# A causal mask for attention scores, set by a minimum on VectorE instead of by products on TensorE

## The chip, the core and the metric

The kernel runs on one core of a Trainium2 chip. It is one launch, and its time is that of the device, in microseconds (us), as the median of several runs. Five engines work side by side, each through its own queue in order: TensorE (PE in the profile, with its weight loads as PEld), VectorE (DVE), ScalarE (ACT), GpSimd (POOL) and SyncE (SP, which issues the loads from memory). They wait for each other through semaphores. TensorE writes its results into PSUM, which has eight banks; all other operands are in SBUF.

## The reference

The program is a decoder trunk of two layers on 256 tokens of width 1024. Each layer is a half-step SwiGLU block, a token mixer and another half-step SwiGLU block, with a norm and a modulation by a condition vector ahead of each. The mixer of the first layer is stick-breaking attention with 16 heads of 64; that of the second is a recurrent block. The change is in the attention alone:

```python
z = jnp.einsum('bhqd,bhkd->bhqk', q[:, :, t0:L], k[:, :, :L])
mask = s_idx[None, :] < t_idx[:, None]
log_keep = jnp.where(mask, jax.nn.log_sigmoid(-z), 0.0)
later = lax.cumsum(log_keep, axis=3, reverse=True) - log_keep
w = jnp.where(mask, jnp.exp(jax.nn.log_sigmoid(z) + later), 0.0)
```

A key that is not earlier than its query gets the weight zero and adds nothing to the running sum. In the kernel both follow when such a score is -1e30: softplus of it is zero, and so is the exponential at the end.

## The kernel before

**Numbers.** Matrix products are made in float32r, with each operand split into a rounded high part and the rest: `wh`, `wl` for weights, two tiles of `hx` for activations. A product is three matmuls (high by high, high by low, low by high), 128x256 results each, and nearly all come from one line, L613 in `group`. ScalarE makes the high part of a weight tile (L584) and VectorE the low part (L587), from a raw tile that SyncE has loaded (`load`).

**Order.** The program is first recorded as a list of operations (`pr.op`), each with an engine, an estimated cost, and the buffers it reads and writes. `Program.schedule` then plays the list through with these costs and decides the order on each engine, and `Space.fit` which bank or tile a buffer gets. So a cost that is changed can move instructions that nothing else in the diff touches. `SCORES` and `VALUES` are the costs given to the score products and the values products.

**Attention** (`attention`) treats the 16 heads as four sets of four heads, c = 0 to 3. Its order is written out by hand as a list of stages: projections of queries and keys (`q`), of values (`v_proj`), then per set `scores`, `sums` and `values`. A set has four score banks, two for each of e = 0, 1. A bank with i = 0 holds scores of the first key block against all 256 queries, for two heads; one with i = 1 holds those of the second key block against the second 128 queries. Keys lie on the partitions, queries along the columns.

For one set the stages follow each other like this:

1. `scores`: per bank one mask product on TensorE (L1104): identity by a mask tile of zeros and -1e30 in bf16, with start=True. It writes the 256 columns where the key block meets the same query block, and the score products (L1119, eight of them on 64 rows of the array) add to it.
2. `softplus`: ScalarE takes absolute values of the banks (two per e, as each bank is ready), an exponential and a logarithm; VectorE adds the positive part of the bank (L1134); then `split` rounds the result into high and low parts, on ScalarE and on VectorE (L877).
3. `sums`: TensorE adds running sums into the same banks, by a triangular matrix (L1149) and, for i = 0, a matrix of minus ones (L1152); ScalarE takes the exponential, which is the weights.
4. `values`: TensorE multiplies weights and values (L1173, on 64 columns of the array); ScalarE and VectorE (L1179) round the result into two parts for the output projection `down`.

Between the stages of a set TensorE has projections of other sets, so that ScalarE and VectorE get time for step 2. VectorE is also given the modulation work: for each tile of the modulation weights, loaded by SyncE into one of four tiles `rawm`, a multiplication with a sum (L647, in `mod_tile`), spread over the blocks by a hook.

At the start of the program GpSimd and VectorE build the constants: `ident`, `ntri`, `none_` and `mask`, which is 256 columns of bf16 (the same 128 columns twice).

Of the kernel before, what the change touches and what calls it, by code (L numbers as in the profile page):

```python
# [14 lines left out]
P = 128  # L15
# [26 lines left out]
KICK0, COPIED, PLAIN = (1, 4), (7,), 2  # L42
HXPAD, HKPAD, ARPAD = 112, 16, 56
SKIP = 1
SCORES = 1400.0
VALUES = 1350.0

OFF_NG = 0
OFF_MB = OFF_NG + 6 * KD
# [359 lines left out]
def trunk(ctx, tc, first_in, cb, par, modw, gu, wdn, qk, wv, wo, win, wri, wout, out):  # L409
# [107 lines left out]
    none_ = fixed("none", P, F32R)  # L517
    dve.tensor_copy(none_, t32[:, P:])
    ident = fixed("ident", P, BF16)
    mask = fixed("mask", T, BF16)  # L520
    pool.affine_select(at[1][:, :P], ones, [[1, P]], ALU.is_equal, 0.0, base=0, channel_multiplier=-1)
    dve.tensor_copy(ident, at[1][:, :P])
    pool.memset(at[2], 0.0)
    for o in (0, P):
        pool.affine_select(at[2][:, o : o + P], at[2][:, o : o + P], [[1, P]], ALU.is_gt, NEG,
                           base=0, channel_multiplier=-1)
    dve.tensor_copy(mask, at[2])
    for t in xbt:
        pool.memset(t[:, 0:4], 0.0)
    mraw, mfin = {}, {}  # L530
# [482 lines left out]
    def attention(l, s, nxt, hook):  # L1013
# [77 lines left out]
        def scores(c):  # L1091
# [3 lines left out]
            pairs = [qs.pop(f) for f in fs]  # L1095
            for e in range(2):
                zs[c, e] = Buf(banks), Buf(banks)

            def masked(b, i):
                def fn():  # L1100
                    diag, m = b()[:, :T], mask
                    if i == 0:
                        diag, m = first(b()), mask.rearrange("p (f t) -> p f t", f=2)
                    pe.matmul(diag, ident, m, start=True, stop=False, skip_group_check=True)  # L1104
                pr.op("PE", c_mm(T, 1), fn, [], [b])

            for e in range(2):
                for i in range(2):
                    masked(zs[c, e][i], i)
            zb = [zs[c, e] for e in range(2)]  # L1110

            def products():

                for j, y in enumerate(pairs):
                    for i, (kc, qc) in enumerate(((slice(T, T + P), slice(0, T)), (slice(T + P, 2 * T), slice(P, T)))):
                        m = NC[i] // 2
                        for e in range(2):
                            rows = slice(e * 64, (e + 1) * 64)
                            pe.matmul(zb[e][i]()[:, j * m : (j + 1) * m], y()[rows, kc], y()[rows, qc], start=False, stop=j == 1,  # L1119
                                      skip_group_check=True)  # L1120

            pr.op("PE", SCORES, products, pairs, [z for zz in zb for z in zz])
            for e in range(2):
                softplus(c, e)

        def softplus(c, e):
# [434 lines left out]
```

## Time and profile before

| | |
|---|---|
| time, median of 3 runs (lowest to highest) | 948.97 us (948.61 to 949.02) |
| the profiled execution: its own time | 950.72 us |
| the profiled execution: span from first to last instruction | 949.0 us |
| mean granted TensorE clock | 0.996 |
| busy: TensorE, VectorE, ScalarE, GpSimd | 938.7, 777.7, 558.9, 2.4 us |
| attention's four score sets, by the mask products | 217.4 to 272.1 us |
| read from memory | 248.92 MB, 263 GB/s over the span |

A row of the timeline gives the start in the span, the length from the first start to the last end, engine, line, operation, tiles out and in, and how many instructions of one kind it holds; a bracket names idle time before it and who ended it. The length of a matmul reaches to the end of its pipeline, so a step on TensorE is read from start to start. A row of the groups gives busy time, the mean length of one in ns, and the idle time ahead of it. A row of the waits names who waited for whom, the total, how often, and the longest. A row of busy time by stage gives, after the stretch and its length, one figure for each engine, then the granted clock, the share of the load engines and GB/s.

### The profile page before, as it was taken

To read this page: it belongs to the slowest core of one execution; us is meant where nothing else is said; L and a number is where in the kernel's file an instruction comes from. 1 tells how busy PE (TensorE), PEld (TensorE's weight loads), DVE (VectorE), ACT (ScalarE), POOL (GpSimd) and SP (SyncE) were. 2 spreads that over 40 slices of the span, in tenths; PEclk is the share of its full clock that TensorE was granted. 3 is DMA by queue.
4 is the path that set the end of the run, shared out by engine and by line. 5 is a ranking of instruction groups with operands and counts; after the bars stand their busy time and mean duration, and the time that the engine had idled before them with its cause. 6 is when DMAs were issued, how large, how long until landed. Compare 5 with 4: busy or idle time off the path is not lost.

```text
span 949.0 us, 19623 instructions
## 1 busy us (share of the span) xinstructions
PE 938.7 (99%) x8094; PEld 927.0 (98%) x8094; DVE 777.7 (82%) x1264; ACT 558.9 (59%) x914; POOL 2.4 (0%) x15
## 2 busy tenths in 40 slices
PE   8999999999999999999999999999999999999997
PEld 6999999999999999999999999999999999999996
DVE  8999988899777998888889998866999997555443
ACT  6785454488775755454367555535789676544343
POOL 1000000000000000000000000000000000000000
PEclk9999999999999999999999999999999999999999
DMA  9989989949643699889967999885253546555431
GB/s 364 404 319 354 346 337 353 365 173 350 235 155 134 242 340 367 311 319 349 362 236 288 344 348 340 333 331 228 90 185 127 223 174 241 208 181 204 171 113 45
DMA packets 48332, 251.25 MB, mean 265 GB/s; under 512 B 5361, under 2 KB 5745, under 8 KB 28530
## 3 DMA queue, kind: packets, MB, share of 16 engines
q1 hardware_dynamic: 47952, 249.59, 69.4%
q8 instruction: 63, 1.03, 0.4%
q10 hardware_dynamic: 290, 0.40, 0.1%
q14 instruction: 27, 0.22, 0.1%
HBM read 248.92 MB, written 1.05 MB: 263 GB/s over the span
## 4 chain that ended last, share of the span: by engine, by line
PE 97%; DMA 1%; DVE 1%; ACT 0%; SPq 0%; DVEq 0%; issue 0%
PE bank L613 90%; PE bank L1044 2%; PE bank L919 1%; PE bank L1279 1%; DMA raw<-in_gu 1%; DMA arenar<-in_first_in 1%; PE bank L1119 1%; PE bank L1173 1%; PE bank L1149 1%; DVE wl L587 0%; DVE arenar L647 0%; DVE x L1391 0%; PE bank L1152 0%; PE bank L1104 0%; PE bank L706 0%; PE bank L698 0%
## 5 line engine op out<-in xcount | busy, mean ns | idle before, releaser
L613 PE MATMUL bank<-hx,wh 128*128 128x256 f32 (+1 forms) x3264 | 560.4, 277 | 0.0
L584 ACT ACTIVATE wh<-raw 128x1024 fp32r<-128x1024 f32 (+1 forms) x330 | 335.3, 1037 | 285.0 <-PE bank L613 196.3
L613 PEld LDWEIGHTS bank<-hx,wh 128*128 128x128 f32 x3264 | 493.3, 188 | 0.0
L587 DVE TENSOR_TENSOR wl<-raw,wh 128x1024 fp32r<-128x1024 f32 (+1 forms) x330 | 387.0, 1196 | 125.6 <-ACT wh L584 121.8
L613 PE MATMUL bank<-hx,wl 128*128 128x256 f32 (+1 forms) x1640 | 452.7, 277 | 0.0
L613 PEld LDWEIGHTS bank<-hx,wl 128*128 128x128 f32 x1640 | 308.4, 188 | 0.0
L613 PE MATMUL bank<-arenar,wh 128*128 128x256 f32 x1696 | 289.8, 276 | 0.0
L613 PEld LDWEIGHTS bank<-arenar,wh 128*128 128x128 f32 x1696 | 255.7, 188 | 0.2 <-issue 0.2
L613 PE MATMUL bank<-arenar,wl 128*128 128x256 f32 x848 | 234.5, 276 | 0.1
L647 DVE SCALAR_TENSOR_TENSOR rawm<-rawm,cact 128x1024 f32<-128x1024 f32 x128 | 154.8, 1220 | 6.3 <-DMA rawm<-in_modw 5.8
L613 PEld LDWEIGHTS bank<-arenar,wl 128*128 128x128 f32 x848 | 159.3, 188 | 0.3 <-DVE wl L587 0.3
L556 ACT ACTIVATE arenar<-a 128x256 fp32r<-128x256 f32 x88 | 35.2, 405 | 9.8 <-DVE a L872 7.9
L877 DVE TENSOR_TENSOR arenar<-a,arenar 128x256 fp32r<-128x256 f32 x88 | 36.5, 419 | 0.5 <-ACT arenar L556 0.5
L556 ACT ACTIVATE sg<-bank 128x256 f32<-128x256 f32 x82 | 30.0, 369 | 10.2 <-PE bank L613 10.2
L872 DVE TENSOR_TENSOR a<-bank,sg 128x256 f32<-128x256 f32 x82 | 34.1, 419 | 1.6 <-ACT sg L556 1.4
L556 ACT ACTIVATE arenaf<-bank 128x256 f32<-128x256 f32 (+1 forms) x53 | 23.3, 487 | 12.5 <-PE bank L613 5.1
L787 DVE SCALAR_TENSOR_TENSOR x<-bank,mf,x 128x256 f32<-128x256 f32 (+1 forms) x49 | 21.7, 474 | 9.3 <-PE bank L613 9.1
L556 ACT ACTIVATE hx<-x,mf 128x256 fp32r<-128x256 f32 x40 | 19.2, 499 | 16.5 <-DVE x L787 16.5
L556 ACT ACTIVATE hx<-hpre,mf 128x256 fp32r<-128x256 f32 x41 | 20.0, 503 | 11.4 <-DVE hpre L733 10.5
L1044 PE MATMUL bank<-wh,hx 128*128 128x256 f32 x128 | 23.0, 279 | 0.0
L647 DVE SCALAR_TENSOR_TENSOR arenar<-arenar,cact 128x1024 f32<-128x1024 f32 x16 | 19.4, 1221 | 1.9 <-DMA arenar<-in_first_in 1.9
L1501 ACT ACT_TABLE_LOAD x15 | 19.2, 1283 | 1.6 <-PEq L1549 1.3
(126 smaller groups left out, 506.5 us busy)
## 6 DMA issues: line engine op xcount, KB each, us to landing
raw<-in_gu SPq DMA_DIRECT2D x79, 1024.0 KB, 5.3
rawm<-in_modw SPq DMA_DIRECT2D x128, 512.0 KB, 6.8
raw<-in_wdn SPq DMA_DIRECT2D x44, 1024.0 KB, 5.1
raw<-in_win SPq DMA_DIRECT2D x10, 1024.0 KB, 4.8
arenar<-in_first_in SPq DMA_DIRECT2D x16, 512.0 KB, 8.4
raw<-in_qk SPq DMA_DIRECT2D x8, 1024.0 KB, 5.0
raw<-in_wout SPq DMA_DIRECT2D x5, 1024.0 KB, 4.8
raw<-in_first_in SPq DMA_DIRECT2D x8, 512.0 KB, 9.3
```

Of the source, the lines that this page charges most:

```text
L556: act.activation(o(), i(), f, **{k: (v() if callable(v) else v) for k, v in kw.items()})
L584: act.activation(h()[:, :m], raw()[:, a : a + m], AF.Copy)
L587: dve.tensor_tensor(lo()[:, :m], raw()[:, a : a + m], f32(h()[:, :m]), ALU.subtract)
L613: pe.matmul(o(b()), wc(u()), xc(v()), start=start and n == 0, stop=stop and n == len(passes) - 1, skip_group_check=True)
L647: dve.scalar_tensor_tensor(raw(), raw(), 1.0, cact(), ALU.mult, ALU.mult, accum_out=m()[:, t : t + 1])
L787: dve.scalar_tensor_tensor(x[d]()[:, w], acc.b()[:, j * T + w.start : j * T + w.stop], gate()[:, d : d + 1], x[d]()[:, w], ALU.mult, ALU.add)
L872: V(lambda: dve.tensor_tensor(a(), b()[:, T:], sg(), ALU.mult), T, [(b, (1, 0)), sg], [a])
L877: V(lambda: dve.tensor_tensor(y[1](), a(), f32(y[0]()), ALU.subtract), n, [a, y[0]], [y[1]])
L919: pr.op("PE", c_mm(T, 4), lambda: pe.matmul(b()[:, g * T : (g + 1) * T], raw()[:, c0 : c0 + P], h0(), start=start, stop=False, skip_group_ ...
L1044: pe.matmul(o, u()[:, tb * P : (tb + 1) * P], v()[:, c0 : c0 + 256], start=start and n == 0, stop=k == KD - 1 and n == 2, skip_group_check ...
L1119: pe.matmul(zb[e][i]()[:, j * m : (j + 1) * m], y()[rows, kc], y()[rows, qc], start=False, stop=j == 1, skip_group_check=True)
L1501: act.preload_act_table_set(TABLES[t])
```

## The change

The mask products are gone. The score products now begin the banks themselves (start=True on the first of the two heads of each bank). When a set's products are done, VectorE takes a minimum in place, bank by bank, of the 256 columns and a mask tile, which holds 1e30 where the key is earlier and -1e30 elsewhere. The mask tile is 128 columns of float32, read twice by an access pattern, and is built with one selection and no cast. The banks are still taken at the same place in the list, by operations on TensorE that cost nothing and issue nothing. `SCORES` and `VALUES` are each 50 larger.

```diff
-SCORES = 1400.0
-VALUES = 1350.0
+SCORES = 1450.0
+VALUES = 1400.0
...
-    mask = fixed("mask", T, BF16)
+    mask = fixed("mask", P)
...
-    pool.memset(at[2], 0.0)
-    for o in (0, P):
-        pool.affine_select(at[2][:, o : o + P], at[2][:, o : o + P], [[1, P]], ALU.is_gt, NEG,
-                           base=0, channel_multiplier=-1)
-    dve.tensor_copy(mask, at[2])
+    pool.memset(mask, -NEG)
+    pool.affine_select(mask, mask, [[1, P]], ALU.is_gt, NEG, base=0, channel_multiplier=-1)
...
-            def masked(b, i):
-                def fn():
-                    diag, m = b()[:, :T], mask
-                    if i == 0:
-                        diag, m = first(b()), mask.rearrange("p (f t) -> p f t", f=2)
-                    pe.matmul(diag, ident, m, start=True, stop=False, skip_group_check=True)
-                pr.op("PE", c_mm(T, 1), fn, [], [b])
-
-            for e in range(2):
-                for i in range(2):
-                    masked(zs[c, e][i], i)
+                for b in zs[c, e]:
+                    pr.op("PE", 0.0, lambda: None, [], [b])
+
...
-                            pe.matmul(zb[e][i]()[:, j * m : (j + 1) * m], y()[rows, kc], y()[rows, qc], start=False, stop=j == 1,
+                            pe.matmul(zb[e][i]()[:, j * m : (j + 1) * m], y()[rows, kc], y()[rows, qc], start=j == 0, stop=j == 1,
...
             for e in range(2):
+                for i in range(2):
+                    b = zs[c, e][i]
+
+                    def masked(b=b, i=i):
+                        o = first(b()) if i == 0 else b()[:, :T].rearrange("p (f t) -> p f t", f=2)
+                        dve.tensor_tensor(o, o, mask.unsqueeze(1).to_broadcast([P, 2, P]), ALU.min)
+                    V(masked, T, [b], [b])
                 softplus(c, e)
```

What the schedule makes of it is seen in the order of the instructions. Line numbers after the change are smaller by 3 ahead of the stage `scores` and by 5 behind it; the score products, L1119, become L1107: L613 becomes L610, L647 L644, L1134 L1129, L877 L874, L1149 L1144, L1152 L1147, L1173 L1168.

TensorE, shortly behind the values products of the second set, where the running sums of the third come (banks 69 and 70 hold the first key block of e = 0 and e = 1; `hk` and `hx` are the activations of a projection of the last queries and keys). Before:

```order
L613 MATMUL bank_68<-hk_95,wh_79 128x256
L613 MATMUL bank_68<-hk_96,wh_79 128x256
L613 MATMUL bank_68<-hk_95,wl_86 128x256
L613 MATMUL bank_68<-hx,wh_79 128x256 x2
L613 MATMUL bank_68<-hx,wl_86 128x256
L613 MATMUL bank_68<-hx,wh_79 128x256 x2
L613 MATMUL bank_68<-hx,wl_86 128x256
L1149 MATMUL bank_69<-arenar_2524,ntri 128x512 x2
```

And now, from the same group on:

```order
L610 MATMUL bank_68<-hk_95,wh_79 128x256
L610 MATMUL bank_68<-hk_96,wh_79 128x256
L610 MATMUL bank_68<-hk_95,wl_86 128x256
L1144 MATMUL bank_69<-arenar_2520,ntri 128x512 x2
L1147 MATMUL bank_69<-arenar_2520,none 128x2x128 x2
L1144 MATMUL bank_65<-arenar_2520,ntri 128x256 x2
L610 MATMUL bank_68<-hx,wh_79 128x256 x2
L610 MATMUL bank_68<-hx,wl_86 128x256
L1144 MATMUL bank_70<-arenar_2520,ntri 128x512 x2
```

(A like group on `hk` stands ahead of the first row shown in both.) Two groups of three matmuls that stood ahead of the first half of the sums now stand behind it, and the second half comes after one further group instead of three. In the fourth set the sums move the other way: the first half two groups later, the second half one.

VectorE, from the last modulation passes ahead of the third set to the end of that set's softplus (`rawm` are modulation tiles, `wl` low parts of weights, bank 69, 65, 70 and 64 the set's score banks). Before:

```order
L647 SCALAR_TENSOR_TENSOR rawm_76,mr_165<-rawm_76,cact 128x1024
L647 SCALAR_TENSOR_TENSOR rawm_77,mr_165<-rawm_77,cact 128x1024
L587 TENSOR_TENSOR wl_89<-raw_73,wh_82 128x1024
L662 TENSOR_TENSOR mr_167<-mr_167,x 128x8
L665 SCALAR_TENSOR_TENSOR mf_168<-mr_167,x 128x8
L1020 TENSOR_TENSOR lam<-lam,nlam 128x10
L1022 TENSOR_SCALAR psp<-lam 128x10
L1021 TENSOR_SCALAR nsp<-lam 128x10
L587 TENSOR_TENSOR wl_90<-raw_71,wh_83 128x1024
L1134 SCALAR_TENSOR_TENSOR arenaf_2525<-bank_69,arenaf_2525 128x512
```

And now:

```order
L644 SCALAR_TENSOR_TENSOR rawm_75,mr_161<-rawm_75,cact 128x1024
L659 TENSOR_TENSOR mr_163<-mr_163,x 128x8
L662 SCALAR_TENSOR_TENSOR mf_164<-mr_163,x 128x8
L1117 TENSOR_TENSOR bank_69<-bank_69,mask 128x2x128
L1117 TENSOR_TENSOR bank_65<-bank_65,mask 128x256
L1117 TENSOR_TENSOR bank_70<-bank_70,mask 128x2x128
L1117 TENSOR_TENSOR bank_64<-bank_64,mask 128x256
L584 TENSOR_TENSOR wl_90<-raw_71,wh_83 128x1024
L644 SCALAR_TENSOR_TENSOR rawm_76,mr_161<-rawm_76,cact 128x1024
L1129 SCALAR_TENSOR_TENSOR arenaf_2521<-bank_69,arenaf_2521 128x512
```

The four minima stand in one piece, directly ahead of a weight split and the softplus additions. Since the first set two modulation passes have moved from ahead of this point to behind it (ten instead of twelve stand ahead, counted from the first set's score products), and the three small passes on `lam` have moved to the first set. SyncE's queue follows: the loads of modulation tiles stand later among the loads of `qk` and `wo` weights.

## The prediction

> **What bounds the kernel now.** I read the page first, then the wait view of TensorE, then the busy time by stage around attention.
>
> ```profile
> span 949.0 us, 19623 instructions
> PE 938.7 (99%) x8094; PEld 927.0 (98%) x8094; DVE 777.7 (82%) x1264; ACT 558.9 (59%) x914; POOL 2.4 (0%) x15
> ...
> PE 97%; DMA 1%; DVE 1%; ACT 0%; SPq 0%; DVEq 0%; issue 0%
> ```
>
> TensorE (PE) is busy for 938.7 of 949.0 us and makes up 97% of the chain that ended last. VectorE (DVE) is busy 82% of the time, so it has room on average, but an average says nothing about attention.
>
> ```profile
> PE bank L919 <- DVE hpre L738: 2.1, 1, 2.1
> PE bank L1412 <- POOL eps L509: 1.2, 1, 1.2
> ```
>
> This is the whole wait view of TensorE: 3.3 us, and L1412 and L919 are warm-up and the first products of the program. Inside attention TensorE waits for nothing. So a product taken from it there is worth its full step, as long as what replaces it keeps TensorE unwaited.
>
> ```profile
> 215.00:245.00 30.00, 30.00 (x264) 28.22 (x263) 29.63 (x41) 25.66 (x43) 0.00 (x0) 1.00 0.89 339
> 245.00:270.00 25.00, 25.00 (x214) 23.53 (x214) 17.08 (x27) 18.41 (x31) 0.00 (x0) 1.00 0.39 136
> 270.00:295.00 25.00, 25.00 (x219) 23.23 (x218) 16.44 (x30) 15.30 (x33) 0.00 (x0) 1.00 0.58 220
> ```
>
> The columns are PE, PEld, DVE, ACT, POOL, then the granted clock. From 215 to 245 us, where the first two of the four score sets lie, VectorE is busy 29.63 of 30 us; in the next two stretches it has 7.9 and 8.6 us free. The clock is 1.00 throughout.
>
> **What TensorE loses.** Sixteen mask products go, four ahead of each score set. Their steps are read from one start to the next, since starts follow each other while one product is still in the pipeline.
>
> ```profile
> 217.29 0.28 PE L613 MATMUL bank<-hx,wl 128*128 128x256 f32 x1
> 217.41 0.61 PE L1104 MATMUL bank<-mask,ident 128*128 128x256 bf16 x4
> 217.95 1.58 PE L1119 MATMUL bank<-arenaf 64*128 64x256 f32 x16
> ...
> 254.77 0.61 PE L1104 MATMUL bank<-mask,ident 128*128 128x256 bf16 x4
> 255.31 1.58 PE L1119 MATMUL bank<-arenaf 64*128 64x256 f32 x16
> ...
> 262.30 0.28 PE L613 MATMUL bank<-hx,wl 128*128 128x256 f32 x1
> 262.51 1.52 PE L1173 MATMUL bank<-arenaf 128*64 128x256 f32 x16
> ...
> 271.45 0.28 PE L613 MATMUL bank<-hx,wl 128*128 128x256 f32 x1
> 271.58 0.61 PE L1104 MATMUL bank<-mask,ident 128*128 128x256 bf16 x4
> 272.12 1.52 PE L1173 MATMUL bank<-arenaf 128*64 128x256 f32 x16
> ```
>
> Each group shown holds the engine for the same 0.54 us from the first mask product to what follows; the second set's stands between the same kinds of products as the third's, and is taken to be like it. Four times 0.54 is 2.16 us, and that is what a first look would take. But one piece of it stays. From the last projection product to the score products it is now 0.66 us (217.29 to 217.95); the row of 262.30 shows what a projection product costs when products on half of the array (64 rows or 64 columns) follow it at once: 0.21 us. In front of the fourth set, too, it is 0.67 us (271.45 to 272.12) and becomes 0.21, since there the values products follow, and the score products come after them as before. So a set gains 0.66 - 0.21 = 0.45 us (0.46 in the fourth; the same for the second and third, whose predecessors are full-array products as well). Four sets: **1.83 us**. I take this and not 2.16, because the row of 262.30 is the very transition that the change creates, only with the other half-array products.
>
> [...]
>
> **What VectorE gains.** Sixteen minima of 128x256 elements, read from a score bank and written back into it, against a mask of 128 columns in SBUF read twice. No row of before writes a bank from VectorE. The nearest rows read one and write SBUF.
>
> ```profile
> L872 DVE TENSOR_TENSOR a<-bank,sg 128x256 f32<-128x256 f32 x82 | 34.1, 419 | 1.6 <-ACT sg L556 1.4
> ...
> 212.80 0.80 DVE L860 SCALAR_TENSOR_TENSOR tr<-bank,rst 128x256 f32<-128x256 f32 x2
> 213.52 3.49 DVE L587 TENSOR_TENSOR wl<-raw,wh 128x1024 fp32r<-128x1024 f32 x3
> ```
>
> One lasts 0.42 us, and the next starts 0.36 us after it (212.80 to 213.52 for two). So a set takes 4 x 0.36 = 1.45 us of VectorE and all sets 5.8 us. Bounds: 0.36 below (the step of a pass over 256 elements that only reads the bank), 0.95 above (a pass over 768 elements, L877 below, in case the write into the bank is slow). I take 0.36.
>
> This lies beside TensorE's work if two covers hold. The first is time between the score products and the products that read their result (L1149, the running sums). The rows show how late VectorE's last part of each chain (L877) was, and when TensorE began to use it:
>
> ```profile
> 228.96 0.95 DVE L877 TENSOR_TENSOR arenar<-arenaf,arenar 128x768 fp32r<-128x768 f32 x1
> 231.35 0.86 PE L1149 MATMUL bank<-arenar,ntri 128*128 128x256 f32 x4
> ...
> 264.04 0.96 DVE L877 TENSOR_TENSOR arenar<-arenaf,arenar 128x768 fp32r<-128x768 f32 x1 [1.57 <-ACT arenar L556]
> 265.72 0.96 DVE L877 TENSOR_TENSOR arenar<-arenaf,arenar 128x768 fp32r<-128x768 f32 x1 [0.72 <-ACT arenar L556]
> 265.47 0.62 PE L1149 MATMUL bank<-arenar,ntri 128*128 128x512 f32 x2
> 267.46 0.62 PE L1149 MATMUL bank<-arenar,ntri 128*128 128x512 f32 x2
> ...
> 280.64 0.95 DVE L877 TENSOR_TENSOR arenar<-arenaf,arenar 128x768 fp32r<-128x768 f32 x1
> 281.70 0.96 DVE L877 TENSOR_TENSOR arenar<-arenaf,arenar 128x768 fp32r<-128x768 f32 x1
> 282.20 0.63 PE L1149 MATMUL bank<-arenar,ntri 128*128 128x512 f32 x2
> 283.49 0.63 PE L1149 MATMUL bank<-arenar,ntri 128*128 128x512 f32 x2
> ```
>
> The spare time is 1.4 us in the first set (229.91 to 231.35), 0.5 and 0.8 in the third, 0.6 and 0.8 in the fourth; the second has some ten. Those are thin, and the order now asks for more: TensorE comes to the third set's sums two projection groups sooner (0.35 us each) and to their second half four groups sooner, besides the masks that are gone.
>
> ```profile
> 218.15 2.01 ACT L584 ACTIVATE wh<-raw 128x1024 fp32r<-128x1024 f32 x2
> ...
> 253.62 0.17 DVE L1021 TENSOR_SCALAR nsp<-lam 128x10 f32<-128x10 f32 x1
> ...
> 256.70 1.36 ACT L556 ACTIVATE arenaf<-bank 128x512 f32<-128x512 f32 x3
> 261.45 1.02 DVE L1134 SCALAR_TENSOR_TENSOR arenaf<-bank,arenaf 128x512 f32<-128x512 f32 x2 [0.59 <-ACT arenaf L556]
> ...
> 274.96 1.36 ACT L556 ACTIVATE arenaf<-bank 128x512 f32<-128x512 f32 x3 [1.40 <-PE bank L1119]
> ```
>
> Third set, worked through. Its score products start at 255.31 - 1.37 = 253.94, and a bank is complete 1.39 later (255.31 to 256.70): 255.33. VectorE had run out of work at 253.79; it now carries eight minima more (2.9 us) and two modulation passes fewer ahead of this point (1.15 each, moved behind), so it is free at 254.4 and waits for the products. Minima from 255.4 to 256.8; ScalarE (ACT) starts its absolute values when the first ends, 255.8 instead of 256.70, and then needs the same 4.75 us up to the second addition (256.70 to 261.45): 260.6, ended at 261.6. ScalarE's rounding of each half now stands ahead of a weight split that it followed before, so the two L877 end at about 262.5 and 263.7. TensorE wants them at 265.47 - 1.37 - 0.70 = 263.4 and 267.46 - 1.37 - 1.41 = 264.7. Spare: about 0.9 and 1.0 us.
>
> Fourth set: absolute values at 273.6 instead of 274.96, as the score products start 1.83 earlier and one minimum lies between. All that follows moves by 1.4: L877 ends near 280.2 and 281.6 (the second 0.3 later still, since the eviction of a value projection now stands ahead of it on ScalarE). The sums come 1.83 earlier, but the order puts two groups more ahead of the first half and one ahead of the second: 281.1 and 282.0. Spare 0.9 and 0.4. First set: ScalarE is busy with weight splits from 218.15 to about 220.1 in any case, and by then the first two minima are over, so the chain starts as before; VectorE ends it about as before, 1.1 us ahead of 231.35 - 0.45. So the stall term is zero, by less than a microsecond at four places. Without this cover each microsecond that a chain is late is one lost.
>
> The second cover is that delayed weight splits and loads come early enough. What is queued behind the minima on VectorE are the splits L587 and the modulation passes L647, and behind those SyncE's loads, which wait for the buffers; two modulation loads that stood ahead of the second wo load now stand between the second and the third, and two more are put ahead of the fourth.
>
> ```profile
> 4.12 0.69 DVE L1446 TENSOR_TENSOR arenaf<-x 128x512 f32<-128x512 f32 x1 [0.73 <-DMA x<-in_first_in]
> ...
> SPq L549 <- DVE wl L587: 105.9, 19, 13.8
> ...
> 288.04 2.01 ACT L584 ACTIVATE wh<-raw 128x1024 fp32r<-128x1024 f32 x2 [1.51 <-PE bank L613]
> ```
>
> The load queue waits 105.9 us in this stretch for free buffers (190 to 330 us), so loads are not the limit there, and the split of the last wo weights waited for TensorE to free its place, not for the load. One to three microseconds of delay cost nothing. The setup passes that change (POOL's selects, a cast on VectorE) cost nothing either: VectorE stood idle before its first pass over data, for the load.
>
> **The sum.** The profiled execution spans 949.0 us and took 950.72; less 1.83 it would be 947.2 and 948.9. The median of the runs is 948.97, which leaves 947.14, **947.1 us**.
>
> **The rivals.** B, *the whole step is gained*: score products follow a projection product without the 0.21. Then 2.16 us go: 946.8. Against it: every change between full and half array in the rows above costs about 0.2. Chance 0.10.
>
> C, *part is given back*: one or two of the places with 0.4 to 1.0 us of spare are overrun, because ScalarE, VectorE and TensorE hand each other more steps than I added up. With 0.4 to 1.5 us of new waits, 0.9 in the middle, the time is 948.0. It speaks for it that the spares are small; against it that VectorE has 8 us free in both later stretches. Chance 0.13.
>
> D, *the minimum in place is slow*, the other side: each set's chain grows by four times what a minimum costs above 0.36. The three tight chains overrun spares of about 1.1, 0.95 and 0.4, 2.45 together; the waits eat the gain when 12 x extra - 2.45 = 1.83, that is from 0.72 us per minimum on. At 0.95 it is 12 x 0.59 - 2.45 = 4.6 us of waits, net +2.8: 951.8. For it speaks only that no row writes a bank this way. Chance 0.12.
>
> **How the numbers follow.** My forecast A has 0.65. Faster or slower counts from 0.2%, 1.9 us, about what a measurement of this kernel can tell from no change; A's 1.83 lies just inside it, and runs of before differ by 0.4 us (948.61 to 949.02), so A falls on either side about evenly: 0.35 faster, 0.30 within. With B faster is 0.45; with C within is 0.43; D alone is slower, 0.12. The range takes in A, B and C: from B less 0.3 for the scatter, 946.5, to C with its whole gain lost, 949.0; D is left out.
>
> **What would show it.** In the profile after: L1104 is gone; the step from L613 to the score products is 0.21; the wait view of TensorE still has its two rows only; minima near 0.42 us, starting 0.36 apart; VectorE nearly without idle time from 215 to 250 us. A new row in TensorE's waits at L1144 (L1149's new number) behind VectorE's L874 would make C right, or D if the minima are long; a step of 0.12 into the score products would make B right.

## The result and the profile after

| | before | changed |
|---|---|---|
| median of 20 runs each | 949.20 us (948.44 to 950.09) | 947.74 us (946.98 to 949.18) |
| profiled execution: time, span | 950.72, 949.0 us | 947.46, 945.7 us |

The ratio is 0.9986 with a 95% interval of 0.9980 to 0.9992: about 1.3 us less, between 0.8 and 1.9. Forecast were 947.1 us (946.5 to 949.0) and a gain of 1.83 us. By the prediction's own line of 1.9 us for "faster" this is "within", to which it had given 0.43 against 0.45.

The page of the changed kernel: span, busy time of each engine, and the chain that ended last by engine.

```profile
span 945.7 us, 19610 instructions
PE 934.8 (99%) x8078; PEld 924.2 (98%) x8078; DVE 781.6 (83%) x1279; ACT 559.3 (59%) x914; POOL 2.1 (0%) x14
...
PE 97%; DVE 2%; DMA 1%; ACT 0%; issue 0%; SPq 0%; DVEq 0%
```

Sixteen products and weight loads are gone (8094 to 8078), and VectorE has 3.9 us more to do. TensorE still makes up 97% of the chain. Its whole wait view (total, times, longest):

```profile
PE bank L916 <- DVE hpre L735: 1.7, 1, 1.7
PE bank L1407 <- POOL eps L509: 1.2, 1, 1.2
PE bank L1421 <- DMA rawm<-in_cb: 0.7, 1, 0.7
```

All three lie in the first 12 us of the program; in attention there is none. Now TensorE's rows at the edges of the first and the fourth score set, where before the mask products stood (L610 is the projection, L1107 the score products, L1168 the values products):

```profile
215.85 0.28 PE L610 MATMUL bank<-hx,wl 128*128 128x256 f32 x1
216.06 0.49 PE L1107 MATMUL bank<-arenaf 64*128 64x256 f32 x2
...
268.66 0.28 PE L610 MATMUL bank<-hx,wl 128*128 128x256 f32 x1
268.87 0.65 PE L1168 MATMUL bank<-arenaf 128*64 128x256 f32 x4
```

From the last full-array product to the first half-array product it is 0.21 us in both (216.06 - 215.85, 268.87 - 268.66), and so it is in the second and third set. Before, 0.66 and 0.67 us went by there. The minima, first all sixteen as a group (shortest, median and longest in ns), then the first set's four in VectorE's timeline:

```profile
L1117 DVE TENSOR_TENSOR bank<-bank,mask x16: 421/423/433, 217.8 to 272.7; 128x256 f32<-128x256 f32 x16
```

```profile
217.77 1.42 DVE L1117 TENSOR_TENSOR bank<-bank,mask 128x256 f32<-128x256 f32 x4
```

Four take 1.42 us, the last of them 0.42: 0.333 from one start to the next. The rows of VectorE and of TensorE that show how early the end of each chain (L874) is for the sums that use it (L1144):

```profile
225.89 0.95 DVE L874 TENSOR_TENSOR arenar<-arenaf,arenar 128x768 fp32r<-128x768 f32 x1
...
227.11 0.96 DVE L874 TENSOR_TENSOR arenar<-arenaf,arenar 128x768 fp32r<-128x768 f32 x1
...
260.06 0.95 DVE L874 TENSOR_TENSOR arenar<-arenaf,arenar 128x768 fp32r<-128x768 f32 x1
261.25 0.96 DVE L874 TENSOR_TENSOR arenar<-arenaf,arenar 128x768 fp32r<-128x768 f32 x1 [0.23 <-ACT arenar L553]
...
277.87 0.95 DVE L874 TENSOR_TENSOR arenar<-arenaf,arenar 128x768 fp32r<-128x768 f32 x1
279.19 0.96 DVE L874 TENSOR_TENSOR arenar<-arenaf,arenar 128x768 fp32r<-128x768 f32 x1 [0.30 <-ACT arenar L553]
```

```profile
228.76 0.62 PE L1144 MATMUL bank<-arenar,ntri 128*128 128x512 f32 x2
...
229.47 0.86 PE L1144 MATMUL bank<-arenar,ntri 128*128 128x256 f32 x4
...
261.99 0.62 PE L1144 MATMUL bank<-arenar,ntri 128*128 128x512 f32 x2
...
263.26 0.62 PE L1144 MATMUL bank<-arenar,ntri 128*128 128x512 f32 x2
...
279.66 0.63 PE L1144 MATMUL bank<-arenar,ntri 128*128 128x512 f32 x2
...
280.36 0.87 PE L1144 MATMUL bank<-arenar,ntri 128*128 128x256 f32 x4
```

Each set has two chains, one for each half (e = 0, 1). Spare time, from the end of L874 to the start of the sums that use it: 1.92 and 1.63 us in the first set (226.84 to 228.76; 228.07 to 229.69), 1.0 and 1.05 in the third (261.01 to 261.99, 262.21 to 263.26), 0.84 and 0.45 in the fourth (278.82 to 279.66; 280.15 to 280.60). The rows of 229.47 and 280.36 hold four products, of which the first two still belong to e = 0; the second chain is needed at the third, at 229.69 and 280.60. Busy time by stage (PE, PEld, DVE, ACT, POOL, clock):

```profile
215.00:245.00 30.00, 30.00 (x264) 28.51 (x264) 29.00 (x47) 26.11 (x42) 0.00 (x0) 1.00 0.83 308
245.00:270.00 25.00, 25.00 (x215) 23.26 (x215) 22.90 (x37) 18.87 (x33) 0.00 (x0) 1.00 0.67 242
270.00:295.00 25.00, 25.00 (x219) 23.79 (x216) 17.14 (x31) 16.42 (x32) 0.00 (x0) 1.00 0.38 146
```

VectorE's first stretch is as full as before (29.00 of 30 us, 29.63 before): eight minima came in and two modulation passes went behind them. The second stretch took both, 17.08 to 22.90.

### The profile page after: what moved, and what is told of

Its sections match the earlier page's. It is cut to its first block, busy times and chain, and to the rows that moved or that the text cites. A ratio compares the mean times of both kernels' runs of the same rounds, so it can differ in the third digit from the quotient of the medians.

```text
span 945.7 us, 19610 instructions
## 1 busy us (share of the span) xinstructions
PE 934.8 (99%) x8078; PEld 924.2 (98%) x8078; DVE 781.6 (83%) x1279; ACT 559.3 (59%) x914; POOL 2.1 (0%) x14
## 3 DMA queue, kind: packets, MB, share of 16 engines
HBM read 248.92 MB, written 1.05 MB: 264 GB/s over the span
## 4 chain that ended last, share of the span: by engine, by line
PE 97%; DVE 2%; DMA 1%; ACT 0%; issue 0%; SPq 0%; DVEq 0%
PE bank L610 90%; PE bank L1041 2%; PE bank L1274 1%; PE bank L916 1%; DMA arenar<-in_first_in 1%; PE bank L1107 1%; PE bank L1168 1%; DVE wl L584 1%; PE bank L1144 1%; DVE arenar L644 0%; DVE x L1386 0%; PE bank L1147 0%; DVE arenaf L1358 0%; PE bank L703 0%; DVE arenaf L1345 0%
## 5 line engine op out<-in xcount | busy, mean ns | idle before, releaser
L610 PE MATMUL bank<-hx,wh 128*128 128x256 f32 (+1 forms) x3264 | 560.4, 277 | 0.0
L610 PEld LDWEIGHTS bank<-hx,wh 128*128 128x128 f32 x3264 | 492.7, 188 | 0.0
L610 PE MATMUL bank<-hx,wl 128*128 128x256 f32 (+1 forms) x1640 | 452.7, 277 | 0.0
L610 PEld LDWEIGHTS bank<-hx,wl 128*128 128x128 f32 x1640 | 308.4, 188 | 0.0
L610 PE MATMUL bank<-arenar,wh 128*128 128x256 f32 x1696 | 289.4, 276 | 0.0
L610 PEld LDWEIGHTS bank<-arenar,wh 128*128 128x128 f32 x1696 | 255.4, 188 | 0.2 <-issue 0.2
L610 PE MATMUL bank<-arenar,wl 128*128 128x256 f32 x848 | 234.3, 276 | 0.1
L644 DVE SCALAR_TENSOR_TENSOR rawm<-rawm,cact 128x1024 f32<-128x1024 f32 x128 | 154.7, 1220 | 8.2 <-DMA rawm<-in_modw 8.2
L610 PEld LDWEIGHTS bank<-arenar,wl 128*128 128x128 f32 x848 | 159.2, 188 | 0.3 <-DVE wl L584 0.3
L553 ACT ACTIVATE arenar<-a 128x256 fp32r<-128x256 f32 x88 | 35.3, 405 | 12.6 <-DVE a L869 10.8
L874 DVE TENSOR_TENSOR arenar<-a,arenar 128x256 fp32r<-128x256 f32 x88 | 36.4, 419 | 0.5 <-ACT arenar L553 0.5
L553 ACT ACTIVATE sg<-bank 128x256 f32<-128x256 f32 x82 | 30.0, 369 | 8.3 <-PE bank L610 8.1
L553 ACT ACTIVATE arenaf<-bank 128x256 f32<-128x256 f32 (+1 forms) x53 | 23.2, 488 | 11.2 <-PE bank L610 5.1
L553 ACT ACTIVATE hx<-x,mf 128x256 fp32r<-128x256 f32 x40 | 19.2, 500 | 16.3 <-DVE x L784 16.3
L553 ACT ACTIVATE hx<-hpre,mf 128x256 fp32r<-128x256 f32 x41 | 20.0, 504 | 11.4 <-DVE hpre L730 10.8
L644 DVE SCALAR_TENSOR_TENSOR arenar<-arenar,cact 128x1024 f32<-128x1024 f32 x16 | 19.5, 1221 | 1.9 <-DMA arenar<-in_first_in 1.9
```

Of the source, the lines that this page charges most:

```text
L553: act.activation(o(), i(), f, **{k: (v() if callable(v) else v) for k, v in kw.items()})
L610: pe.matmul(o(b()), wc(u()), xc(v()), start=start and n == 0, stop=stop and n == len(passes) - 1, skip_group_check=True)
L644: dve.scalar_tensor_tensor(raw(), raw(), 1.0, cact(), ALU.mult, ALU.mult, accum_out=m()[:, t : t + 1])
L874: V(lambda: dve.tensor_tensor(y[1](), a(), f32(y[0]()), ALU.subtract), n, [a, y[0]], [y[1]])
```

## Where the two profiles differ, and how much of it is the change

The two profiled executions differ by 3.26 us, twice the gain forecast, so I compared every start of TensorE in the one with its counterpart in the other (the mask products left out). The lead of the changed kernel arises in three places only: 1.44 us in the first 17 us of the program, 1.81 us in attention, 0.37 us between 750 and 760 us. The middle one falls in four steps at the four places forecast: 0.452, 0.454, 0.454 and 0.454 us. (They make 3.62 us; 0.35 us of it is lost again behind TensorE's last product.) The first and the last lie far from any minimum or mask product. So both kernels were run again unchanged, the kernel before three times and the changed one twice. What the expectations call the mode switch is the step of 0.21 us from a full-array to a half-array product, in place of 0.12 between two full-array ones (215.85 to 216.06 and 215.51 to 215.63 in the changed kernel).

> The changed kernel once more, unchanged. By the theory of the mode switch (four steps of 0.45 us are gone from the attention part, and nothing else of the change reaches TensorE) the offsets of TensorE's starts against the first profile of the kernel before fall by 1.81 us in the attention part, at the same four places, within 0.02 us each. What lies outside it, 1.44 us in the first 20 us and 0.37 us between 750 and 760 us, is expected to come out otherwise, since these two have no instruction of the change near them. Rival: these two belong to the change (the loads that it moves at the start); then they come back with the same sizes. Time by the theory: 1.8 us under the kernel before, give or take the start's 1.4; ratio 0.998.

> The kernel before once more, unchanged. By the theory that the start's 1.44 us and the 0.37 us at 750 us are scatter from one execution to the next, its starts differ from those of its own first profile by amounts of this size at such places (up to 1.5 us in the first 20 us, some tenths in stretches of projection products), and by under 0.02 us across the four places in the attention part. Rival: the two kernels differ in the start; then this run repeats the first profile within 0.1 us everywhere.

> The kernel before, unchanged, for the two differences outside the attention part. By the theory that they are scatter of single executions, TensorE's pause ahead of its first products at L919, 2.06 and 1.92 us in the two profiles so far, comes out below 1.7 us in one of this run and the next as it did in six of eight runs of the changed code (1.13 to 1.68), and then the products behind it run at full rate and TensorE stands 1.3 us earlier; and the hundred products between 750 and 760 us come at 0.113 us each in one of the two, 0.37 us less. Rival: both belong to the order that the change moved; then this run has a pause of over 1.9 us and 0.118 us a product once more.

> The same once more: with four profiles of the kernel before, all four with a pause of over 1.9 us and 0.118 us a product would speak for the rival, one at the other value of either for scatter in that one.

> The changed kernel, unchanged, timed once more. By the theory of the mode switch its time is 1.8 us under the kernel before, and up to 2.2 us if the 0.118 us a product between 750 and 760 us is what the kernel before always does; ratio 0.9977 to 0.9981. In the attention part TensorE's starts against the kernel before fall by 1.81 us once more. By rival C (a part of the gain is given back) the ratio is over 0.999.

Measured, as the time from one of TensorE's products to a later one. The products are numbered without the mask products; a product of unsplit float32 operands, which left two records 0.216 us apart in the trace (L919), counts once. In the first profile of the kernel before, products 60, 1600, 2400, 6000 and 7000 start at 22.58, 197.39, 299.47, 716.36 and 831.25 us, so 1600 to 2400 encloses attention and 6000 to 7000 the stretch at 750 us. A product of L919 or L916 at half rate took twice its usual step, 0.85 us in place of 0.43:

| profile | pause ahead of L919 / L916 | half-rate products behind it | product 60 at | 60 to 1600 | 1600 to 2400 | 6000 to 7000 |
|---|---|---|---|---|---|---|
| before, first | 2.06 | 4 | 22.58 | 174.81 | 102.079 | 114.89 |
| before_again | 1.92 | 4 | 22.46 | 174.81 | 102.079 | 114.89 |
| before_third | 1.36 | 0 | 20.07 | 175.26 | 102.079 | 114.92 |
| before_fourth | 1.13 | 0 | 19.94 | 175.50 | 102.079 | 114.53 |
| changed, first | 1.68 | 0 | 21.15 | 174.81 | 100.265 | 114.53 |
| after_again | 1.13 | 0 | 20.00 | 175.96 | 100.265 | 114.53 |
| after_third | 1.73 | 0 | 20.58 | 175.53 | 100.266 | 114.88 |

The column of attention is the same to the nanosecond in four profiles of the one and within one in three of the other, and differs by **1.814 us**. Everything from 2400 to 6000 is the same in all seven (416.89 us). The column of 6000 to 7000 takes both its values in both kernels, and before_third and before_fourth start without half-rate products, as the changed kernel does: my rival that the start and the stretch at 750 us belong to the change fell with them. The half-rate start does not need the old code either, since two kernels with the new one, min_none and last_x2 (below), have it. It came in two of four profiles of the kernel before and in two of nine of the changed kernel and its variants; whether it is as frequent in both is not shown. The two places can be seen in the windows of the kernel before, the first profile and then before_fourth:

```profile
11.50:16.00 4.50, 4.50 (x14) 3.70 (x15) 3.96 (x8) 1.43 (x5) 0.00 (x0) 0.65 1.03 405
745.00:765.00 20.00, 19.88 (x169) 19.69 (x169) 19.63 (x42) 15.43 (x33) 0.00 (x0) 1.00 0.41 159
```

```profile
11.50:16.00 4.50, 4.50 (x22) 3.97 (x21) 3.85 (x8) 2.46 (x6) 0.00 (x0) 1.00 1.03 397
745.00:765.00 20.00, 19.90 (x171) 19.70 (x170) 19.82 (x42) 16.63 (x35) 0.00 (x0) 1.00 0.50 180
```

In the first the granted clock is 0.65 from 11.5 to 16 us and fourteen records of products lie in this stretch; in the second it is 1.00 and there are twenty-two. What this scatter does to the time: before_again took 950.62 us, before_third 948.68 and before_fourth 948.44, one program. It is as large as the whole gain, which is why the time alone says little: after_again had 947.57 us (one of its eleven executions took 955.63) against 949.80 (ratio 0.9986, 0.9971 to 1.0001), after_third 947.85 against 948.84 (0.9986, 0.9977 to 0.9995). A gain of 1.81 us is a ratio of 0.9981; all three intervals hold it.

## Experiment: one half of the change

The first two sets are masked by products again, the last two by minima.

```diff
+BYPE = (0, 1)
...
+                    if c in BYPE:
+                        pr.op("PE", c_mm(T, 1), product, [], [b])
...
-                            pe.matmul(..., start=j == 0, stop=j == 1,
+                            pe.matmul(..., start=j == 0 and c not in BYPE, stop=j == 1,
...
-                for i in range(2):
+                for i in range(2 if c not in BYPE else 0):
```

> The first two sets are masked by TensorE's products, as before the change, the last two by minima. By the theory of the mode switch a set is worth 0.454 us by itself: against the changed kernel TensorE starts 0.454 us later behind the first set and 0.908 behind the second, and no more behind the third and the fourth; into the score products it takes 0.21 us in the last two. Rival: the gain is of the whole (VectorE's or the planner's order); then the steps are spread otherwise. Between 750 and 760 us, where the kernel before took 0.118 us a product and the changed one 0.113, it may go either way, by 0.36 us: a wait of some 0.28 us for a weight lies ahead of it, and the products seem to keep the rhythm in which they start again.

TensorE's timeline in this kernel, ahead of the first and of the third set (L617 is its projection, L1107 its mask product, L1122 its score product, L1159 a sum):

```profile
215.37 0.28 PE L617 MATMUL bank<-hx,wl 128*128 128x256 f32 x1
215.48 0.61 PE L1107 MATMUL bank<-maskb,ident 128*128 128x256 bf16 x4
216.02 0.49 PE L1122 MATMUL bank<-arenaf 64*128 64x256 f32 x2
...
252.38 0.63 PE L1159 MATMUL bank<-arenar,ntri 128*128 128x256 f32 x4
252.94 0.49 PE L1122 MATMUL bank<-arenaf 64*128 64x256 f32 x2
```

0.65 us from projection to scores (215.37 to 216.02) where a product masks, and nothing between sums and scores where a minimum does. The steps against the changed kernel are 0.452 behind the first set and 0.454 behind the second, then none; against the kernel before none in the first two, and 0.453 and 0.454 in the last two. Products 1600 to 2400 take 101.159 us, halfway (102.079, 100.265). So the gain belongs to the single set and adds up. This is one profile, of an execution of 947.49 us, which by itself would not show it.

## Experiment: no minima at all

```diff
-                        dve.tensor_tensor(o, o, mask.unsqueeze(1).to_broadcast([P, 2, P]), ALU.min)
+                        return
```

> The changed kernel without its sixteen minima; the causal mask is left out of the computation, all else and the order of instructions stay. By the theory that the minima are wholly hidden TensorE's starts in the attention part are those of the changed kernel within 0.1 us, and the time is equal to it (0.1 us of 948); only the spares change, by up to 1.4 us to the better for the score parts of each set. Rival: the minima cost TensorE something that no wait row shows (their writes to score banks beside its products, or the delay of what VectorE does next); then this kernel is faster by that, 0.3 to 1.8 us, and the change would have given back a part.

Products 1600 to 2400 take 100.266 us, as in the changed kernel (100.265), with VectorE 4.6 us less busy (777.0 against 781.6). No step of 0.06 us or more lies between the two anywhere behind 17 us. So the sixteen minima cost TensorE nothing: neither their writes into banks beside its products nor the delay of what stands behind them on VectorE. The time was 947.07 us against 949.80 (0.9971, 0.9961 to 0.9982); the changed kernel had 947.57 beside it (after_again). That min_none's median is 0.5 us lower is not the minima's doing as far as the traces show: they are equal where the minima are. Its profiled execution even had the half-rate start (1.4 us later at product 60).

## Experiments: longer chains

Each minimum issued four times, twice, and twice in the fourth set alone. The result stays, and so does the order of all other instructions.

```diff
-                        dve.tensor_tensor(o, o, mask.unsqueeze(1).to_broadcast([P, 2, P]), ALU.min)
+                        for _ in range(4): dve.tensor_tensor(o, o, mask.unsqueeze(1).to_broadcast([P, 2, P]), ALU.min)
```

with `range(2)` in min_x2 and `range(1 + (c == 3))` in last_x2.

> Each of the sixteen minima is issued four times in place; the values are the same, and the order of instructions too. Twelve more steps of 0.333 us for each set, 4.0 us. By the theory (the minima stand in a chain whose end has spares of 1.9 us in the first set, 10 in the second, 1.2 in the third, 0.7 in the fourth) TensorE now waits ahead of the products that use the softplus of the sets, at L1144, behind VectorE's L874, by up to 2.1, 0, 2.8 and 3.3 us: 8 us in all if the chain is delayed by the whole 4.0, and some 2.5 if ScalarE's work on the first two banks takes up the half of it. Rival: VectorE has room beyond what the chain shows and nothing waits; then the time is that of the changed kernel. Other rival: VectorE's later work (projections' evictions) is what becomes late; then the new rows are at L610 for banks, not at L1144.

Measured: 968.18 us, 20 more; products 1600 to 2400 take 121.62 us, 21.35 more than in the changed kernel. No theory had that. VectorE's minima of the first and the third set in the fourfold kernel, then TensorE's waits in attention:

```profile
217.51 7.03 DVE L1117 TENSOR_TENSOR bank<-bank,mask 128x256 f32<-128x256 f32 x16
...
262.59 7.03 DVE L1117 TENSOR_TENSOR bank<-bank,mask 128x256 f32<-128x256 f32 x16
```

```profile
PE bank L1144 <- ACT arenar L553: 10.5, 3, 7.2
PE bank L1144 <- DVE arenar L874: 2.8, 3, 2.4
```

Three things were mis-sized. A set grew by 5.6 us (7.03 - 1.42), not 4.0: a minimum on the bank that the one ahead of it has just written starts 0.467 us behind it, on another bank 0.34. Second, lateness carries over. VectorE has next to no idle time between 217.5 and 269.5 us; the third set's minima begin at 262.59, although TensorE's score products were done by 258.3 (253.91 in the changed kernel, plus the 4.4 us by which TensorE is late there). So the 7.15 us of wait in the third set are in good part the second set's minima, whose own spare of ten microseconds hid them from TensorE but not from VectorE. Third, waits are 13.3 us of 21.35; most of the other 8 us are products at half rate behind each of the three long waits. TensorE's rows that end the waits, and windows behind them (the clock is third from the end):

```profile
231.86 0.79 PE L1144 MATMUL bank<-arenar,ntri 128*128 128x512 f32 x1 [2.41 <-DVE arenar L874]
273.75 0.79 PE L1144 MATMUL bank<-arenar,ntri 128*128 128x512 f32 x1 [7.15 <-ACT arenar L553]
297.73 0.80 PE L1144 MATMUL bank<-arenar,ntri 128*128 128x512 f32 x1 [3.06 <-ACT arenar L553]
```

```profile
232.00:236.00 4.00, 4.00 (x21) 3.44 (x23) 4.00 (x6) 4.00 (x8) 0.00 (x0) 0.59 0.23 62
273.00:277.00 4.00, 3.05 (x10) 2.46 (x11) 3.68 (x5) 4.00 (x8) 0.00 (x0) 0.50 0.34 121
297.00:301.00 4.00, 3.08 (x8) 2.30 (x9) 3.72 (x6) 4.00 (x7) 0.00 (x0) 0.50 0.00 0
```

The place was as expected (L1144, behind the softplus; no new row at L610), and the second set had none. Most of the waiting ended with ScalarE's half of the split (L553, 10.5 us), not with VectorE's L874 (2.8): ScalarE works on the banks when their minima are done, so it is late with them.

> Each of the sixteen minima is issued twice in place; the values are the same. With the 0.44 us that the fourfold run showed from one minimum to the next on the same bank, a set's minima take 3.5 us instead of 1.42: 2.1 us more, about what rival D had for a slow minimum (0.95 us each). By the theory that VectorE's lateness carries over from set to set: waits at L1144 of 0 to 0.9 us in the first set, none in the second, about 2 us in the third (1.7 carried over, 2.1 of its own, 1.6 of idle time used up before it, 1.2 of spare less some of ScalarE's), 0.5 to 1.5 us in the fourth; TensorE 2.5 to 4.5 us later than in the changed kernel, and more by up to 3 us behind a wait of over 2 us, since the fourfold run had half-rate products there. By the theory of sets that stand alone, as the prediction had it (2.1 against spares of 1.9, 10, 1.2 and 0.7): 0.2, 0, 0.9 and 1.4 us, 2.5 us in all. By rival A's reading that there is room everywhere: the time of the changed kernel.

> Only the four minima of the fourth set are issued twice; the values are the same. 2.1 us more ahead of a spare of 0.7 us (0.5 more is idle time of VectorE inside the chain). If a wait costs its own length: one new wait row at L1144 of 0.9 to 1.4 us, and TensorE ends that much later than in the changed kernel. If a wait of about 1 us also brings half-rate products behind it, as 2.7 us did in the fourfold run: 1.5 to 3 us more on top. If a short wait changes the rhythm of the products behind it (0.118 in place of 0.113 us), up to 0.4 us on top. All steps up to 278 us are those of the changed kernel.

VectorE's four doubled minima in the fourth set, in min_x2 and then in last_x2, and TensorE's waits at L1144 in min_x2:

```profile
272.88 3.30 DVE L1117 TENSOR_TENSOR bank<-bank,mask 128x256 f32<-128x256 f32 x8 [0.60 <-PE bank L1107]
```

```profile
273.41 3.30 DVE L1117 TENSOR_TENSOR bank<-bank,mask 128x256 f32<-128x256 f32 x8 [0.75 <-PE bank L1107]
```

```profile
PE bank L1144 <- ACT arenar L553: 0.7, 1, 0.7
PE bank L1144 <- DVE arenar L874: 0.5, 1, 0.5
```

In min_x2 a set grew by 1.9 us (3.30 - 1.43). TensorE lost nothing in the first two sets, 1.57 us in the third and 0.56 in the fourth, 2.14 in all between products 1600 and 2400, and 0.29 behind them, up to product 3000, in products at a slower pace. Sets that stand alone would have given the third 0.9 and the fourth 1.4: carrying over is right, its sizes were a little high. In last_x2 TensorE lost 0.70 us, under the 0.9 to 1.4 expected, and too little at a time for a row in the wait view (0.12 and 0.07 us idle at L1144): of the 1.87 us that the chain grew by, 0.53 went into VectorE's idle time ahead of the second L1129, and 0.68 into the spare, counted up to the product that needs VectorE's half, which leaves 0.66. Neither run had half-rate products in attention; the waits were 0.7 us and less. A short wait costs more than the idle time in its row, which is counted from the end of the product ahead, 0.28 us behind its start: a row of 0.66 us was 0.82 us from start to start (min_x2), idle time of 0.12 us was 0.28 (last_x2), and the product behind came 0.1 us later still. The times, one execution each, were 949.46 us (min_x2) and 949.53 (last_x2, with the half-rate start).

## Experiment: half-array blocks side by side

If a switch between full-array and half-array products costs what the traces say, fewer switches must gain. The second set's scores are issued directly ahead of the first set's values.

```diff
         sums(0, 1)
-        scores(1)
         q(4)
+        scores(1)
         values(0)
```

> The changed kernel with the scores of the second set issued directly ahead of the values of the first, so that two blocks of half-array products adjoin: one step into and one out of full-array products go. By the price of a switch in the traces (0.21 us in place of 0.113 on the way in, some 0.1 on the first product behind it) TensorE is 0.1 to 0.25 us ahead of the changed kernel behind 245 us, if the second set's spare, 10 us, stays over the 5 us by which its scores move. Rival: the switch is paid between the two kinds of half-array products as well (64 rows contracted there, 64 columns here), and nothing is gained; or VectorE, which then has the second set's minima later among its weight splits, comes late at L1144 in the second or third set, by some tenths to 2 us. The time by itself can't tell 0.2 us from nothing.

TensorE's timeline of this kernel, then the same values products of the changed kernel, then scores followed by a projection in the kernel before:

```profile
235.90 0.28 PE L610 MATMUL bank<-hx,wl 128*128 128x256 f32 x1
236.11 1.58 PE L1107 MATMUL bank<-arenaf 64*128 64x256 f32 x16
237.62 1.52 PE L1168 MATMUL bank<-arenaf 128*64 128x256 f32 x16
239.07 0.50 PE L610 MATMUL bank<-hk,wh 128*128 128x256 f32 x2
```

```profile
237.73 0.28 PE L610 MATMUL bank<-hx,wl 128*128 128x256 f32 x1
237.93 1.52 PE L1168 MATMUL bank<-arenaf 128*64 128x256 f32 x16
239.38 0.50 PE L610 MATMUL bank<-hk,wh 128*128 128x256 f32 x2
```

```profile
233.07 1.58 PE L1119 MATMUL bank<-arenaf 64*128 64x256 f32 x16
234.58 0.50 PE L613 MATMUL bank<-hk,wh 128*128 128x256 f32 x2
```

Products 1600 to 2400 take 100.065 us, 0.200 less than in the changed kernel, and there is no wait in attention. The rival was right in its first half: the switch is paid between the two kinds of half-array products too. From the first score product to what follows it is 1.51 us whether values come next (236.11 to 237.62) or a projection (233.07 to 234.58), although the last score product is one of those that otherwise take 0.10 us to the next and here took 0.20; and the values block takes 1.45 us behind scores as behind a projection (237.62 to 239.07, 237.93 to 239.38). What is gained is one switch: into scores, out, into values and out are four, and into scores, over to values and out are three. The time was 947.26 us against 949.27 (0.9985, 0.9976 to 0.9994). By the traces this beats both kernels; by the time it can't be told from the changed one, as was expected.

## Why the prediction was right, step by step

- **TensorE sets the end.** It held: 97% of the chain before and after, and what came off its steps in attention came off the end: every product from 2400 to 6000 stands at the same distance in all seven profiles.
- **The switch stays when the mask products go: 0.45 us a set, 1.83 in all.** Measured 0.452 to 0.454 and 1.814. (The four terms as written, three times 0.45 and 0.46, add up to 1.81; the 1.83 was a slip of the sum.) The row of 262.30 that I took for a transition the trace didn't have (0.21) was the right one: 0.206 to 0.211. late agrees with it: one change of array shape less gained 0.20 us, and from the first score product to what followed it was 1.51 us both to the other half-array products and to full-array ones. Why a change of shape costs this was not shown.
- **Rival B** (2.16 us, a step of 0.12) is out by that row.
- **The minimum: 0.42 us long, 0.36 apart.** Measured 0.423 and 0.333; a set takes 1.42 us where I had 1.45. **Rival D**, a slow write into the bank, is out by the same row. Its price would have come near at a small size, in part by luck: at 0.80 us a minimum (0.46 + 0.34, min_x2) its sum gives 12 x (0.80 - 0.36) - 2.45 = 2.8 us, measured were 2.1 in attention and 0.3 behind it. But by set it has 0.7, 0.8 and 1.4 us in the first, third and fourth, and 0, 1.57 and 0.56 came. At 1.73 us (min_x4) it gives 14.0, and 21.35 came, because it let sets stand alone and products run at full rate behind a wait.
- **Spares of 1.1, 0.9 and 1.0, 0.9 and 0.4 us, so no stall.** Measured 1.63 (the tighter of the first set's two), 1.0 and 1.05, 0.84 and 0.45. The first set's figure was read against a row that begins with products of the other half: they need the second chain 0.23 us later, and 231.35 - 0.45 - 229.91 is 0.99, not 1.1. **Rival C** is out: there is no wait row in attention, and min_none, without the minima, is no faster in attention.
- **Loads and weight splits 1 to 3 us later cost nothing.** min_none shows it for the splits and all else behind the minima on VectorE; no row of TensorE's waits names a weight split or a load in attention.
- **The time.** 947.74 instead of 947.1. The step behind it was right to 0.02 us; the base was not: the median of three runs that I took off from, 948.97, was 949.20 over twenty, and the profiled execution of before had a start that cost two microseconds. 0.4 us of the remaining gap is inside the scatter of the start.
- Of what was to be seen in the profile after, one thing came otherwise: a third row in the wait view, L1421 for the load of the conditions, 0.7 us. after_again doesn't have it, so it is scatter too.

## What to carry to other kernels

Price a removed instruction by the step between its neighbours that remains, not by its own length, and look for a row where those neighbours already meet: it gave 0.45 here against 0.54, and 0.454 was measured. Where blocks of different array shapes meet, count the changes of shape, also those between two half-array shapes: here one less gained 0.20 us (late). When a change is smaller than the scatter of the times, compare starts of the bounding engine between two instructions that enclose the change, over several profiles of both kernels: the distance was the same within 1 ns while the times spread by two microseconds. A helper engine that runs without idle time can hand a delay on to a later stage that has less spare (in min_x4 TensorE waited for nothing in the second set and 7.15 us in the third), so spares can't be added up set by set.

## What the runs showed of the hardware

**Pauses of 1.89 us and more were followed by half rate, those of 1.73 us and less were not.** Ahead of L919 or L916 TensorE waits for the first normalized rows. In the thirteen profiles at hand the pause was 1.13, 1.13, 1.13, 1.14, 1.36, 1.44, 1.52, 1.68 and 1.73 us without any effect, and 1.89 (min_none), 1.92, 2.06 and 2.28 us (last_x2) with four products of 0.85 us in place of 0.43 behind it. In the middle of the program the waits of 2.41, 3.06 and 7.15 us of min_x4 did the same, for 3.4 to 5.9 us behind their end (granted clock 0.59, 0.50 and 0.50 in the windows shown with them), and those of 0.7 us in min_x2 didn't (1.00 from 261 to 265 us). The first products behind a pause could still run at full rate: in the first profile of the kernel before the pause ended at 11.46 us, the granted clock was 1.00 from there to 12.83 us, 0.50 from 12.83 to 16.25 and 1.00 again behind it. What sets the start and the length of such a stretch, and whether the length of the pause alone decides, was not shown.

**Near 750 us products came at one of two paces for the length of a group.** Every profile has a step of 0.36 to 0.40 us, in place of 0.113, there to the first product with a fresh weight split. Some eighty products behind it, as far as the next change of operands, then came 0.1178 us apart in five of the thirteen profiles and 0.1133 in eight, in both kernels; that is the 0.36 us. In after_again a step of 0.48 us near 36 us left the slower pace for 150 products; but in after_third the same products had the slower pace behind a step only 0.06 us longer than usual, and in before_fourth the faster one behind a step of 0.55. The length of the step doesn't decide near 750 us either: steps of 0.361 to 0.387 us went with the faster pace, 0.367 to 0.397 with the slower one. What does stays open.

**Minima on one bank in a row were slower than on four banks in turn:** 0.46 to 0.47 us from start to start (min_x2, min_x4) against 0.333, each 0.42 to 0.43 us long. The repeated minimum also reads what the one ahead of it wrote; which of the two counts was not separated.
